# Attention scores of a hybrid streaming encoder: from two 64-row products per head to one 128-row product with both halves of the keys stacked

## The chip, the cores and the metric

The kernel runs on one core of one Trainium2 chip. The metric is the time of one execution on the device, in microseconds (us). The core has a matrix engine (PE, TensorE), whose weight loads the profile lists apart as PEld, a vector engine (DVE), a scalar engine (ACT), a slower general engine (POOL, GpSimd) and a queue that issues DMAs (SP). Each engine runs its own instructions in order and waits on semaphores for the others. On-chip working memory (SBUF) has 128 partitions; matrix products land in eight banks of PSUM.

## The reference

Two layers. In each, 1024 frames of a new stream (the prompt) and 32 frames of a running stream (the sample) are normalised, projected by one wide matrix and fed to three branches: A, a gated mixing inside chunks of 128; B, sliding-window attention with 8 query heads that share 2 key heads; C, chunk-band attention with 4 heads over the own chunk of 64 and 8 chunks before it. Gates multiply the branch outputs, and a second projection, a normalisation and a residual follow. Head width is 64. What the change touches is this (for the prompt):

```python
def block_attention(q, k, v, bias, valid, sinks):
    s = jnp.einsum('bnqhgd,bnlhd->bnhgql', q, k) * (HEAD_DIM ** -0.5) + bias
    if valid is not None:
        s = jnp.where(valid[None, :, None, None, None, :], s, NEG_INF)
    if sinks is None:
        p = jax.nn.softmax(s, axis=-1)
    else:
        m = jnp.maximum(jnp.max(s, axis=-1, keepdims=True), sink)
        e = jnp.exp(s - m)
        p = e / (jnp.sum(e, axis=-1, keepdims=True) + jnp.exp(sink - m))
    return jnp.einsum('bnhgql,bnlhd->bnqhgd', p, v)
```

## The kernel before

**Precision.** PE multiplies a rounded 32-bit format (float32r, printed fp32r) at full rate. To keep the accuracy of float32, an operand x is split into a high part (x rounded) and a low part (x minus the high part); `split` (line 420) does this with a copy on ACT or DVE and a subtraction on DVE or POOL. A product of two split operands is the sum of high by high, high by low and low by high: three matmuls.

**Stages.** A layer has two. In the first, 24 blocks of 128 projection columns (named `bq0`, `ck1`, `cz0` and so on; the order is written out in `ORDERS`, line 40) are computed for three token ranges of 384, 384 and 288 columns (`TOK`): 24 dense matmuls of 128 rows each, into one of three accumulator banks `d`, evacuated by `evac` (line 593). Queries are evacuated, scaled by 1/8, into the big tile `Y`, two heads of 64 on the 128 partitions. Keys are evacuated into a tile `v`, stored, and split (line 613) into `kt[:, 0]` (high) and `kt[:, 1]` (low), again two heads on the partitions. Gate blocks (`bz`, `cz`) are evacuated only when the attention of their pair is done. In the second stage the output projection runs over the three token ranges.

**Attention.** It is woven into the first stage. A `Unit` (line 650) is one pair of heads and a run of query blocks of 128: four blocks in branch B, two in C (`NQ`, line 53), so 8 units of B and 8 of C in a layer. Block q sees 1 or 2 key tiles of 128 in B and 1 to 5 in C. A unit has these steps:

- `Q(h)`: split of 256 query columns (two blocks) of both heads.
- `scores` (line 751): both heads j = 0, 1 from partitions 0 to 63 and 64 to 127, each into its own bank `S` (there are two), three matmuls of 64 rows each, alternating between the heads (`mm_s`, `both`). In B one call does two blocks, in C one; with five key tiles a call `tails` does the second half of the keys. Then DVE adds the bias and takes the minimum of the negated score (the op shows as CUSTOM_DVE_ANT_0), and `softmax` does the exponential on ACT, the sum with the sink in B, a reciprocal and a scaling.
- `T(g)`: transposes of the probabilities by PE into a bank `pt`, split into `ph` and `pl`. The last one of a head releases its score tiles `s`.
- `PV(g)`: products with the values into `pv`; at the end one half is copied to a tile `ot` by ACT and added to the other by DVE into `Y`.

Score tiles `s` come from a ring of 6 (`BUFS`, line 63); B takes 2 for two blocks, C 2 for a block.

**Order.** The whole program is written out by a planner when it is built: `Clock` (line 87) keeps an assumed time for each engine and buffer, steps wait in lanes (`LANES`, line 69), and `pump` (line 1118) takes a step when its assumed time has come, and otherwise lets the next dense matmul go. Nothing is reordered at run time. All engine instructions pass through one helper, so nearly every row of the profile has its line, L282, and is told apart by its tiles: `S<-kk,qh` is a score product with the high part of the queries, `d<-hh,whi` a dense one.

Of the kernel before, what the change touches and what calls it, by code (L numbers as in the profile page):

```python
# [40 lines left out]
    "bk bv bq0 cv0 bq1 ck1 bq2 bq3 av1 bz2 ck0 av0 cq0 cv1 cq1 az0 au0 bz0 bz1 bz3 az1 au1 cz1 cz0".split(),  # L41
    "bk bv bq0 bq2 bq1 ck1 bq3 cv0 av0 bz2 ck0 av1 cq0 cv1 au0 bz1 cq1 az0 bz0 cz0 bz3 az1 au1 cz1".split(),
# [21 lines left out]
    tmp=3, v=5, r=3, wraw=3, whi=3, wlo=3, kk=2, vv=2, ks=3, vs=3, s=6, qh=2, ql=2, ph=2, pl=2,  # L64
    nm=3, sm=3, sx=2, rd=3, ot=1, bias=3, t5=1, d=3, S=2, pt=2, pv=1,
# [4 lines left out]
    "wload store evac ysplit wsplit x h0 sq0 h1 sq1 h2 sq2 bnd0 bnd1 bnd2 xl lc t5 bias p t sb a vt sc q s"  # L70
# [227 lines left out]
def encoder(  # L298
# [158 lines left out]
    sk4 = cp.tile([128, 4, 2, 2], F32, name="sk4")  # L457
# [135 lines left out]
    def evac(l, n, t, d):  # L593
# [8 lines left out]
        elif ty == "k" or (ty == "v" and br != "a"):  # L602
# [47 lines left out]
    class Unit:  # L650


        def __init__(self, l, br, pair, qp):
# [23 lines left out]
            self.qh, self.ql, self.s, self.pt = {}, {}, {}, {}  # L677
# [3 lines left out]
        def steps(self):  # L681
            l, u = self.l, self
            halves = self.nq // 2
            for h in range(halves):
                end = self.c0 + 256 * h + 255
                tok = end // 384
                q = f"{l}.{self.br}q{self.pair}.{tok}"
                src = Y[:, self.blk, end - 255 : end + 1]
                lane("q").put(lambda h=h: self.Q(h), lambda q=q: q in done and free("qh") and free("ql"),
                              lambda src=src: max(after("act", [src]), slot("qh", "act")), f"{self.id}.Q{h}")  # L690
                need = marks(f"{self.id}.Q{h}", *(f"{l}.{self.k}.{t}" for t in range(tok + 1)), f"{l}.{self.br}{self.pair}.bias")
                parts = self.parts(h)
                for i, (p, fresh) in enumerate(parts):
                    done_h = i == len(parts) - 1

                    def part(p=p, h=h, done_h=done_h):
                        p()
                        if done_h:
                            let_go(u.qh[h], u.ql[h])
                            if u.end and h == halves - 1:  # L700
# [724 lines left out]
```

## Time and profile before

| | |
|---|---|
| time, median of 3 runs | 1029.36 us (1028.28 to 1031.23) |
| time of the profiled execution | 1028.7 us |
| its span, first to last instruction | 1027.0 us |
| mean granted clock of PE, share of full speed | 0.995 |
| busy: PE, DVE, ACT, POOL | 98%, 70%, 50%, 6% of the span |
| chain of work that ended last, by engine | PE 72%, DVE 13%, ACT 8%, issue 4%, DMA 2% |

How to read what follows. In a timeline a row has the start in us, a duration in us, engine, line, operation, the tiles as out<-in, the part of the array used and the shape of the moving operand, and a count of merged instructions. Matmuls are pipelined: their durations overlap, and what one costs is the distance from its start to the next start. A row of windows has the stretch in us, its length, then for PE, PEld, DVE, ACT and POOL the busy time and in brackets the number of instructions, then the granted clock of PE as a share of 2.4 GHz, the busy share of the DMA engines, and GB/s. A row of one tile has the count, durations in ns as min/median/max, first and last start in us, and the shapes. A row of groups has the count, then total busy us and mean ns of one, then the idle time before and who ended it.

### The profile page before, as it was taken

The page shows a single profiled execution, that of the slowest core. Times are in us where ns is not written, and L with a number is a line of the kernel's source. Part 1 is how long each engine was busy: PE and PEld are TensorE (multiplying, and loading weights), DVE is VectorE, ACT ScalarE, POOL GpSimd, SP SyncE. Part 2 cuts the span into 40 slices and gives each one's busy share as a digit, 9 for nine tenths or more (in the row PEclk, how much of TensorE's full clock was granted, in tenths as well). Part 3 has the DMA queues.
Part 4 walks back from the last instruction along what each step waited for, and adds up shares of the span by engine and source line. Part 5 has one row for each costly group of instructions (what it writes and reads, how often), then busy time and mean ns, then how long its engine had stood idle before and what let it go on. Part 6 is the DMA issues. An engine that isn't in the chain of part 4 may idle for free.

```text
span 1027.0 us, 18406 instructions
## 1 busy us (share of the span) xinstructions
PE 1003.7 (98%) x6842; PEld 951.4 (93%) x6842; DVE 715.6 (70%) x1849; ACT 509.5 (50%) x1300; POOL 66.6 (6%) x146
## 2 busy tenths in 40 slices
PE   8999999999999999999999999999999999999995
PEld 7899999988999999999988989899889899999995
DVE  8676777757677745857977687776676776566655
ACT  7465556435555512645744555653564454246331
POOL 0200100110000000000010010001100000000000
PEclk9999999999999999999999999999999999999998
DMA  8211111101100311435542110201011003126633
GB/s 279 44 55 43 43 42 47 53 21 39 63 21 22 114 42 63 157 119 183 161 125 67 32 56 29 68 22 61 25 32 57 32 21 94 41 83 196 190 101 120
DMA packets 52634, 78.63 MB, mean 77 GB/s; under 512 B 7104, under 2 KB 28992, under 8 KB 52544
## 3 DMA queue, kind: packets, MB, share of 16 engines
q1 hardware_dynamic: 52544, 77.45, 24.3%
q8 instruction: 54, 0.88, 0.4%
q14 instruction: 36, 0.29, 0.1%
HBM read 66.11 MB, written 11.31 MB: 75 GB/s over the span
## 4 chain that ended last, share of the span: by engine, by line
PE 72%; DVE 13%; ACT 8%; issue 4%; DMA 2%; POOL 0%; SPq 0%; POOLq 0%; ACTq 0%; DVEq 0%
PE d L282 47%; PE S L282 12%; PE pt L282 7%; PE pv L282 5%; ACT s L282 4%; DVE Y L282 3%; DVE pl L282 2%; DVE v L282 1%; DVE s L282 1%; DVE kk L282 1%; DVE wlo L282 1%; ACT ph L282 1%; DVE hl L282 1%; DMA wraw<-in_wo_dram 1%; ACT ot L282 1%
## 5 line engine op out<-in xcount | busy, mean ns | idle before, releaser
L282 PE MATMUL d<-hh,whi 128*128 128x384 f32 (+1 forms) x1132 | 382.4, 338 | 0.1
L282 PE MATMUL d<-hh,wlo 128*128 128x384 f32 (+1 forms) x1132 | 365.9, 323 | 0.8 <-DVE wlo L282 0.7
L282 PE MATMUL d<-hl,whi 128*128 128x384 f32 (+1 forms) x1132 | 364.9, 322 | 0.0
L282 PEld LDWEIGHTS d<-hh,whi 128*128 128x128 f32 x1132 | 213.0, 188 | 13.9 <-issue 8.4
L282 PEld LDWEIGHTS d<-hh,wlo 128*128 128x128 f32 x1132 | 212.7, 188 | 1.9 <-DVE wlo L282 1.9
L282 PEld LDWEIGHTS d<-hl,whi 128*128 128x128 f32 x1132 | 213.6, 189 | 0.0
L282 ACT ACTIVATE s<-s,nm 128x256 f32<-128x256 f32 (+5 forms) x196 | 107.8, 551 | 107.1 <-DVE nm L282 107.0
L282 DVE TENSOR_TENSOR pl<-pt,ph 128x512 fp32r<-128x512 f32 (+2 forms) x136 | 80.7, 623 | 18.0 <-ACT ph L282 17.6
L282 DVE TENSOR_TENSOR wlo<-wraw,whi 128x512 fp32r<-128x512 f32 x108 | 76.9, 714 | 6.5 <-ACT whi L282 5.0
L282 ACT ACTIVATE ph<-pt 128x512 fp32r<-128x512 f32 (+2 forms) x136 | 68.4, 541 | 23.3 <-PE pt L282 22.4
L282 ACT ACTIVATE whi<-wraw 128x512 fp32r<-128x512 f32 x105 | 65.2, 626 | 20.7 <-PE d L282 13.0
L282 PE MATMUL pv<-pl,vv 128*128 128x256 f32 (+1 forms) x288 | 70.2, 284 | 2.0 <-DVE pl L282 2.0
L282 ACT ACTIVATE ot<-pv 64x256 f32<-64x256 f32 x96 | 36.3, 378 | 71.1 <-PE pv L282 37.7
L282 PE MATMUL pv<-ph,vv 128*128 128x256 f32 (+1 forms) x288 | 70.2, 272 | 1.3 <-ACT ph L282 1.1
L282 ACT ACTIVATE tmp<-tmp 128x384 f32<-128x384 f32 (+1 forms) x48 | 23.9, 498 | 88.5 <-DVE tmp L282 85.0
L282 PE MATMUL pt<-ident,s 128*128 128x128 f32 x488 | 67.6, 274 | 0.0
L282 DVE TENSOR_TENSOR Y<-pv,ot 64x256 f32<-64x256 f32 x96 | 40.4, 421 | 36.2 <-ACT ot L282 35.2
L282 DVE CUSTOM_DVE_ANT_0 s<-S,bias,nsink 128x256 f32<-128x256 f32 (+1 forms) x128 | 52.1, 464 | 9.5 <-PE S L282 6.7
L282 DVE TENSOR_TENSOR v<-v,tmp 128x384 f32<-128x384 f32 (+1 forms) x80 | 41.7, 522 | 24.4 <-ACT tmp L282 23.3
L282 PEld LDWEIGHTS pv<-pl,vv 128*128 128x128 f32 x288 | 54.4, 189 | 3.9 <-DVE pl L282 3.6
L282 PEld LDWEIGHTS pt<-ident,s 128*128 128x128 f32 x488 | 56.0, 140 | 1.4 <-DVE s L282 0.2
L282 PEld LDWEIGHTS pv<-ph,vv 128*128 128x128 f32 x288 | 54.4, 189 | 2.7 <-ACT ph L282 1.8
(169 smaller groups left out, 1677.8 us busy)
## 6 DMA issues: line engine op xcount, KB each, us to landing
wraw<-in_w_dram SPq DMA_DIRECT2D x96, 256.0 KB, 2.7
wraw<-in_wo_dram SPq DMA_DIRECT2D x72, 256.0 KB, 3.0
x_d<-Y SPq DMA_DIRECT2D x16, 192.0 KB, 3.2
out_y_dram<-Y SPq DMA_DIRECT2D x16, 192.0 KB, 3.8
Y<-in_xT_dram SPq DMA_DIRECT2D x5, 576.0 KB, 6.1
bias<-fc_d SPq DMA_DIRECT2D x8, 320.0 KB, 4.3
s<-in_xT_dram SPq DMA_DIRECT2D x12, 192.0 KB, 3.2
s<-x_d SPq DMA_DIRECT2D x12, 192.0 KB, 3.9
```

Source lines behind the costliest of these rows:

```text
L282: return f(*args, **kw)
```

## The change

Scores use the full height of the array. For each head j the key tile holds the high part on one half of the partitions and the low part on the other: `kt[own, j]` and `kt[other, j]`. The queries of a head are put on both halves by four DMAs (`D`, in a new lane `qd`), from `Y` into the first 256 columns of the score tile that the block will use anyway, and split there. One matmul with the queries' high part then gives high by high plus high by low, and a second with the low part adds low by high and low by low: two matmuls of 128 rows instead of three of 64. All steps are per block of 128 queries: the split, the scores (in B both heads in one bank, in C one head at a time, with one or two banks) and the softmax. `softmax`, `tails` and `both` go into `scores`. A block takes its score tiles (one in B, two in C) when its query DMAs are issued. Besides, the copy before the last addition of `PV` goes to the shared ring `tmp` instead of `ot`, `qh` and `ql` have 3 buffers instead of 2, `v` 4 instead of 5, the expanded sink tile `sk4` is gone, and `ORDERS` is another.

```diff
@@ ORDERS @@
-    "bk bv bq0 cv0 bq1 ck1 bq2 bq3 av1 bz2 ck0 av0 cq0 cv1 cq1 az0 au0 bz0 bz1 bz3 az1 au1 cz1 cz0".split(),
-    "bk bv bq0 bq2 bq1 ck1 bq3 cv0 av0 bz2 ck0 av1 cq0 cv1 au0 bz1 cq1 az0 bz0 cz0 bz3 az1 au1 cz1".split(),
+    "bk bv bq0 bq1 cv0 ck1 bq2 cq0 av1 bq3 bz2 av0 cq1 ck0 bz3 az0 bz0 cv1 au1 au0 az1 bz1 cz0 cz1".split(),
+    "bk bv bq0 bq1 bq2 cv0 ck1 av0 bq3 av1 bz2 ck0 cq0 cq1 bz0 au1 cv1 bz1 au0 az1 az0 bz3 cz1 cz0".split(),
@@ BUFS @@
-    tmp=3, v=5, ... qh=2, ql=2, ... ot=1, ...
+    tmp=3, v=4, ... qh=3, ql=3, ...
@@ evac, keys @@
-                split(kt[:, 0, a : a + P], kt[:, 1, a : a + P], x[:, :P])
+                for j in (0, 1):
+                    own, other = slice(64 * j, 64 * j + 64), slice(64 - 64 * j, 128 - 64 * j)
+                    split(kt[own, j, a : a + P], kt[other, j, a : a + P], x[own, :P])
@@ Unit @@
+        def D(self, q):
+            c = self.c0 + 128 * q
+            self.t[q] = [tl([128, 640], "s") for _ in range(1 if self.br == "b" else 2)]
+            self.qr[q] = self.t[q][0][:, 0:256].rearrange("p (j c) -> p j c", j=2)
+            src = Y[:, self.blk, c : c + 128]
+            for j in (0, 1):
+                for i in (0, 1):
+                    dma.dma_start(self.qr[q][64 * i : 64 * i + 64, j, :], src[64 * j : 64 * j + 64, :])
+
-        def Q(self, h):
-            c = self.c0 + 256 * h
-            self.qh[h] = tl([128, 256], "qh", F32R)
-            self.ql[h] = tl([128, 256], "ql", F32R)
-            split(self.qh[h], self.ql[h], Y[:, self.blk, c : c + 256])
+        def Q(self, q):
+            self.qh[q] = tl([128, 2, 128], "qh", F32R)
+            self.ql[q] = tl([128, 2, 128], "ql", F32R)
+            split(self.qh[q], self.ql[q], self.qr[q])
         def mm_s(self, dst, j, q, c0, c1):
...
-            yield lambda: pe.matmul(dst, qh[sl, qs], kt[sl, 0, lo + c0 : lo + c1], start=True, stop=False)
-            yield lambda: pe.matmul(dst, qh[sl, qs], kt[sl, 1, lo + c0 : lo + c1], start=False, stop=False)
-            yield lambda: pe.matmul(dst, ql[sl, qs], kt[sl, 0, lo + c0 : lo + c1], start=False, stop=True)
+            k = st[self.l, self.k][:, j, 128 * self.lo[q] + c0 : 128 * self.lo[q] + c1]
+            pe.matmul(dst, self.qh[q][:, j, :], k, start=True, stop=False)
+            pe.matmul(dst, self.ql[q][:, j, :], k, start=False, stop=True)
+        def parts(self, q):
             if self.br == "b":
-                return [(lambda: self.scores((2 * h, 2 * h + 1)), True)]
...
+                return [(lambda: self.scores(q, (0, 1)), 1)]
+            return [(lambda j=j: self.scores(q, (j,)), 1 if self.n[q] <= 4 else 2) for j in (0, 1)]
+        def scores(self, q, js):
+            s = self.t[q][js[0]]
...
+            for c in range(0, n, m):
+                bank = ps("S")
+                for i, j in enumerate(js):
+                    dst = bank[:, 256 * i : 256 * i + m]
+                    self.mm_s(dst, j, q, c, c + m)
...
             if self.br == "b":
-                dve.tensor_tensor(sx, nm, sk4[:, self.pair, :, :].rearrange("p j q -> p (j q)"), ALU.add)
-                act.activation(sx, sx, AF.Exp)
-                dve.tensor_tensor(sm, sm, sx, ALU.add)
+                dve.tensor_tensor(sx[:, :2], nm[:, :2], sinkb[:, self.pair : self.pair + 5 : 4], ALU.add)
+                act.activation(sx[:, :2], sx[:, :2], AF.Exp)
+                dve.tensor_tensor(sm[:, :2], sm[:, :2], sx[:, :2], ALU.add)
             rd = tl([128, 4], "rd")
-            dve.reciprocal(rd[:, :nb], sm[:, :nb])
-            for b, k in enumerate(blocks):
-                scale(self.s[k], rd[:, b : b + 1])
+            dve.reciprocal(rd[:, :2], sm[:, :2])
+            for j in (0, 1):
+                scale(self.s[j, q], rd[:, j : j + 1])
@@ PV @@
-                    ot = tl([128, 256], "ot")
+                    ot = tmp()[:, :256]
```

## Rows read from the trace of the kernel before

**Rows 1.** The page, busy time, share of the span and instructions of each engine.

```profile
PE 1003.7 (98%) x6842; PEld 951.4 (93%) x6842; DVE 715.6 (70%) x1849; ACT 509.5 (50%) x1300; POOL 66.6 (6%) x146
```

**Rows 2.** Windows: attention of layer 0, dense rest, attention of layer 1, dense rest.

```profile
45.60:362.60 317.00, 314.13 (x2249) 291.31 (x2249) 226.18 (x669) 169.53 (x465) 23.05 (x57) 1.00 0.16 48
365.30:414.50 49.20, 49.20 (x312) 49.20 (x312) 27.26 (x52) 12.00 (x26) 0.20 (x1) 1.00 0.17 54
532.10:874.60 342.50, 339.31 (x2414) 316.11 (x2414) 244.45 (x705) 176.34 (x480) 23.05 (x43) 1.00 0.15 46
874.60:916.70 42.10, 42.10 (x269) 41.61 (x268) 23.61 (x46) 11.49 (x25) 2.59 (x2) 1.00 0.15 51
```

**Rows 3.** One tile, the queries' high part, whole span.

```profile
L282 PE MATMUL S<-kk,qh x448: 270/307/502, 45.6 to 854.9; 64*128 64x256 f32 x81, 64*128 64x320 f32 x44, 64*128 64x128 f32 x15, 64*128 64x384 f32 x6
L282 ACT ACTIVATE qh<-Y x42: 399/404/420, 29.3 to 806.5; 128x256 fp32r<-128x256 f32 x42
L282 DVE TENSOR_TENSOR ql<-Y,qh x40: 410/423/456, 30.9 to 816.2; 128x256 fp32r<-128x256 f32 x40
```

**Rows 4.** Timeline of PE, a call of B's scores between dense matmuls.

```profile
130.02 0.34 PE L282 MATMUL d<-hh,wlo 128*128 128x384 f32 x1
130.29 0.50 PE L282 MATMUL S<-kk,qh 64*128 64x256 f32 x4
...
131.19 0.44 PE L282 MATMUL d<-hh,whi 128*128 128x384 f32 x1
131.47 0.34 PE L282 MATMUL d<-hl,whi 128*128 128x384 f32 x1
131.64 0.34 PE L282 MATMUL d<-hh,wlo 128*128 128x384 f32 x1
```

**Rows 5.** Timeline of PE, a call of C's scores on 320 keys.

```profile
749.83 0.29 PE L282 MATMUL d<-hh,wlo 128*128 128x288 f32 x1
750.05 0.56 PE L282 MATMUL S<-kk,qh 64*128 64x320 f32 x4
750.45 0.31 PE L282 MATMUL S<-kk,ql 64*128 64x320 f32 x2
750.69 0.40 PE L282 MATMUL d<-hh,whi 128*128 128x288 f32 x1
750.92 0.29 PE L282 MATMUL d<-hl,whi 128*128 128x288 f32 x1
751.06 0.30 PE L282 MATMUL d<-hh,wlo 128*128 128x288 f32 x1
```

**Rows 6.** Timeline of PE, four products with the values between dense matmuls.

```profile
336.86 0.34 PE L282 MATMUL d<-hh,wlo 128*128 128x384 f32 x1
337.03 0.28 PE L282 MATMUL pv<-ph,vv 128*128 128x256 f32 x1
...
337.50 0.34 PE L282 MATMUL d<-hh,whi 128*128 128x384 f32 x1
337.68 0.34 PE L282 MATMUL d<-hl,whi 128*128 128x384 f32 x1
```

**Rows 7.** One tile, the keys: the low part, whole span.

```profile
L282 DVE TENSOR_TENSOR kk<-v,kk x18: 425/559/1524, 27.0 to 701.1; 128x384 fp32r<-128x384 f32 x12, 128x256 fp32r<-128x256 f32 x6
```

**Rows 8.** Groups by line, the softmax's reciprocal.

```profile
L282 DVE RECIPROCAL rd<-sm 128x4 f32<-128x4 f32 (+2 forms) x70 | 12.0, 171 | 37.9 <-ACT s L282 34.8 <-ACT vv L282 1.8
```

**Rows 9.** Timeline of the SP queue, eight small DMAs one after another.

```profile
25.16 3.68 SPq L282 DMA_DIRECT2D ssk<-in_sinks_dram  x8
```

**Rows 10.** DMA issues: count, KB each, median us from issue to landing.

```profile
bias<-fb_d SPq DMA_DIRECT2D x16, 20.0 KB, 2.6
ssk<-in_sinks_dram SPq DMA_DIRECT2D x16, 0.1 KB, 1.7
```

**Rows 11.** Timeline of PE, transposes that free four score tiles, then scores.

```profile
105.12 0.95 PE L282 MATMUL pt<-ident,s 128*128 128x128 f32 x7
106.00 0.50 PE L282 MATMUL S<-kk,qh 64*128 64x256 f32 x4
```

More of the change, by code (lines that the diff above doesn't have):

```diff
@@ L682, in steps, with part @@
             l, u = self.l, self
-            halves = self.nq // 2
-            for h in range(halves):
-                end = self.c0 + 256 * h + 255
+            for q in range(self.nq):
+                end = self.c0 + 128 * q + 127
                 tok = end // 384
[L687 to L696, printed above, removed]
-                        p()
-                        if done_h:
-                            let_go(u.qh[h], u.ql[h])
-                            if u.end and h == halves - 1:
+                there = f"{l}.{self.br}q{self.pair}.{tok}"
+                src = Y[:, self.blk, end - 127 : end + 1]
+                tiles = 1 if self.br == "b" else 2
+                lane("qd").put(lambda q=q: self.D(q), lambda there=there, tiles=tiles: there in done and free("s", tiles),
+                               lambda src=src, tiles=tiles: max(after("dma", [src]), slot("s", "dma", tiles)), f"{self.id}.D{q}")
+                lane("q").put(lambda q=q: self.Q(q), lambda d=f"{self.id}.D{q}": d in done and free("qh") and free("ql"),
+                              lambda q=q: max(after("act", [self.qr[q]]), slot("qh", "act")), f"{self.id}.Q{q}")
+                need = marks(f"{self.id}.Q{q}", *(f"{l}.{self.k}.{t}" for t in range(tok + 1)), f"{l}.{self.br}{self.pair}.bias")
+                parts = self.parts(q)
+                for i, (p, banks) in enumerate(parts):
+                    done_q = i == len(parts) - 1
+                    def part(p=p, q=q, done_q=done_q):
+                        p()
+                        if done_q:
+                            let_go(u.qh[q], u.ql[q])
+                            if u.end and q == u.nq - 1:
                                 let_go(*st[l, u.br, u.pair, "bias"])
@@ L703, in part @@
                                     let_go(st[l, u.k])
-                    lane("s").put(part, lambda fresh=fresh, need=need: need() and free("S", 2) and (not fresh or free("s", 2)),
-                                  lambda h=h: max(after("pe", [u.qh[h], u.ql[h]]), slot("S", "pe", 2)),
-                                  f"{self.id}.S{h}" if done_h else None, True)
+                    lane("s").put(part, lambda banks=banks, need=need: need() and free("S", banks),
+                                  lambda q=q, banks=banks: max(after("pe", [u.qh[q], u.ql[q]]), slot("S", "pe", banks)),
+                                  f"{self.id}.S{q}" if done_q else None, True)
             for i, g in enumerate(self.groups):
                 qs = {q for _, q0, n in g[1] for q in range(q0, q0 + n)}
-                vneed = marks(*(f"{self.id}.S{q // 2}" for q in qs))
+                vneed = marks(*(f"{self.id}.S{q}" for q in qs))
                 lane("t").put(lambda g=g: self.T(g), lambda vneed=vneed: vneed() and free("ph") and free("pl"),
```

90 lines of the change are left out of this document (27 added, 63 removed).

## The prediction

> **What bounds the kernel now.** I read the page's busy line first. The matrix engine (PE) is busy 98% of the span, the vector engine (DVE) 70%, the scalar engine (ACT) 50% [rows 1]. A busy PE need not be a PE that lacks time, so the second view is the windows. I cut each layer where its attention ends: from the first to the last attention matmul of layer 0 and of layer 1, and behind each the stretch of projection blocks that is left over before the output projection starts. In the attention stretches PE idles 317.00 - 314.13 = 2.9 us and 342.50 - 339.31 = 3.2 us, together 6.1 us, at a granted clock of 1.00 (the upper level, 2.4 GHz); DVE is busy 226.18 of 317.00 and 244.45 of 342.50 us, 71% in both [rows 2]. So PE's instruction stream sets the time: dense projection matmuls fill every hole that attention leaves, and a microsecond taken out of PE's stream is a microsecond off the end, as long as nothing else gets late. The other two windows are the cover for lateness: attention is finished 49.2 us before the dense blocks run out in layer 0, and 42.1 us in layer 1 [rows 2].
>
> The third view is the timeline of PE alone, because durations of matmuls overlap and only the distance from start to start is what one of them costs. There the scores show a price that no duration shows, at their two borders with the dense work; the next part takes it apart.
>
> **Score matmuls: removed and added.** The trace has 448 products with the high part of the queries [rows 3], and two of these go with one of the low part [rows 5], so 672 in all. By the code they come as 32 calls of branch B (12 each: two query blocks, two heads, three products) and 48 calls of branch C (6 each).
>
> A B call: the last dense start before it comes 0.27 us ahead of the first score where two dense neighbours of that size stand 0.17 apart, so 0.10 goes on the way in. From the first score to the next dense start it takes 131.19 - 130.29 = 0.90. The first dense step afterwards is 0.28 instead of 0.17, 0.11 on the way out [rows 4]. Sum 1.11 us. A C call on 320 keys: 0.22 against 0.14 on the way in, 750.69 - 750.05 = 0.64 inside, 0.23 against 0.14 on the way out [rows 5]. Sum 0.08 + 0.64 + 0.09 = 0.81 us.
>
> The new scores contract over all 128 rows, in the form that the probability-times-value products have now: 128 rows, rounded f32, two products in a row into the same bank. Four of these on 256 columns between dense neighbours take 337.50 - 337.03 = 0.47, that is 0.1175 each, and the dense steps on both sides stay at 0.17 and 0.18 [rows 6]: no price at the borders. A B call becomes 8 such products (two blocks, two heads, two products): 8 x 0.1175 = 0.94. Saved 1.11 - 0.94 = 0.17 a call, 32 x 0.17 = 5.4 us. A C call of 6 on 320 columns becomes 4. At 320 columns the step lies halfway between 0.1175 for 256 [rows 6] and 0.17 for 384 [rows 4], 0.147 by the slope: 4 x 0.147 = 0.59. Saved 0.81 - 0.59 = 0.22, 48 x 0.22 = 10.6 us; the 16 C calls of other widths are taken at the same saving, since the borders make it up. Together 16.0 us. All of it is border: inside, 0.94 replaces 0.90 and 0.59 replaces 0.64.
>
> Here a rule of the Trainium skill stands against the change. "TensorEngine Tiling (Array Packing)", section Overview, gives products with at most 64 rows up to twice the throughput, since two sit side by side in the array; going to 128 rows gives that up. By it alone the 12 old products would be six slots of 0.1175, 0.71 us, and the change would cost 8 slots, 0.94: +0.23 x 32 for B and, in the same way, +0.15 x 48 for C, 14.6 us slower. The trace does not bear that out at the level of a call: 0.90 plus borders, not 0.71. The same page, section Key Properties, says that a change of tiling mode drains the engine, and the 0.10 and 0.11 at the borders agree. The sum goes by the rows.
>
> **Query splits.** Before, 48 splits of 256 columns, one for two blocks; after, 96 of 256 columns, since each block now stands on both halves. 48 more high parts at 0.404 us, mostly on ACT, and 48 more low parts at 0.423 us, mostly on DVE [rows 3]: 19.4 us on ACT, 20.3 on DVE.
>
> **Key splits.** Each of 18 becomes two, of half the partitions and the same columns. A row of DVE costs 0.56 [rows 7]; taking high and low part alike, 18 x 2 x 0.56 = 20 us more. If fewer partitions were quicker it would be zero; no row shows that, so I keep 20.
>
> **Softmax per block.** Exponentials and bias additions keep count and width. For B the sink's two small additions and the reciprocal come 64 times instead of 32: 32 x 3 x 0.171 [rows 8] = 16 us on DVE, plus 32 small exponentials on ACT.
>
> DVE gets 20 + 20 + 16 = 57 us, 28 in each attention stretch, which is itself 8 us shorter: (226 + 28) / 309 = 82% and (244 + 28) / 334 = 82%, from 71%. ACT goes from 170 to about 183 of 309. Neither passes PE; the cover is PE's dense work. But the handover waits behind the 6.1 us of PE idle grow when the queues are fuller. If they go as busy over idle share, 0.71/0.29 = 2.4 becomes 0.82/0.18 = 4.6, and 6.1 becomes 11.5: plus 5 us. Bounds: nothing, or three times that (15).
>
> **The query DMAs.** 96 blocks x 4 = 384 new DMAs on the SP queue, behind which weight loads wait. Eight small ones took 3.68 us there, 0.46 each [rows 9], so four take 1.8; small ones land 1.7 to 2.6 us after issue [rows 10]. With the split, 0.4 + 0.4, a block's queries are ready 4.3 to 5.2 us after its tile comes free; I take 4.8. SP's queue grows by 177 us; in its own list of waits it mostly waits for a free weight buffer, so this is hidden, and weight loads, of which three are buffered, stand behind a query DMA that waits for its tile or for the evacuated queries. On ACT the query split now waits for the landing, and behind it stand exponentials and weight splits, for which PE waits in turn; the planner places it by an assumed landing time. If that time is kept, the chain alone matters: the score tile (6 of them) is now taken before the DMA. Today the score follows the last transposes that free its tile at once (transposes from 105.12, score at 106.00) [rows 11]; in the timeline the same happens once per pair of heads in B and once per unit in C, 4 + 8 = 12 times a layer. The 4.8 us come in there: 12 x 4.8 = 58 us of lateness a layer, less what the finer blocks give back. The cover is 49.2 + 8 = 57 and 42.1 + 8 = 50. I price it at nothing in the sum, with little to spare.
>
> The reordered blocks, the copy through the shared temporary instead of its own tile, and one buffer less for evacuated rows change no instruction's cost; each lies under dense work and gets zero, with an unknown of a few us either way that is inside the bounds above.
>
> **Sum.** The profiled execution took 1028.7 us (span 1027.0, the rest around it), 0.7 below the median of 1029.36. 1028.7 - 16.0 + 5 = 1017.7; beside the median 1018.4. I say 1018.
>
> **Rivals.** (a) *Vector work eats the gain.* PE's idle grows by 15 instead of 5: 1028.7 - 16 + 15 = 1028. For it: DVE is already the releaser of handovers, and 82% is an average over busier stretches. Against: only 6.1 us idle at 71%. Chance 0.17, of which 0.08 still faster, 0.07 same, 0.02 slower.
> (b) *The borders stay.* If the 0.2 us per call comes with any change to another operand pattern and not with the 64-row form, the change does not do what it says: 16.0 falls to 48 x 0.05 - 32 x 0.04 = 1, and about 1028 without any growth of waits, 1033 with it. Against: [rows 6] has none. Chance 0.06, mostly same.
> (c) *Attention comes too late; slower.* Place: the last heads of branch C, whose gate blocks end each layer and hold the accumulator banks until attention is there. Price: 4.8 us per exposed refill. It decides from 12 refills in layer 0 (57 us) and 10 in layer 1 (50 us) on; beyond, PE idles one for one. With 14 refills a layer, 67 us: 10 + 17 = 27 us lost, 1018 + 27 = 1045; 16 in each would lose 20 + 27. For it: [rows 11], and the cover matches the need so nearly. Against: two tiles of six are free for the next unit's first blocks; one block's softmax is a shorter chain than two's. Chance 0.17: 0.15 slower, 0.01 same, 0.01 faster. "DMA: Bandwidth & Descriptors", Rules for kernel authors, in the Trainium skill advises against two transfers to disjoint halves of the partitions, since they share the same engines and serialize; no run before shows such a pair. By it the four transfers of a block would land one behind another, which only lengthens the wait that (c) needs.
>
> **How the numbers follow.** A measurement of this kernel tells about 0.3%, 3 us, from no change. Forecast 0.60, all faster, its own range 1009 (no growth of waits, somewhat fewer than today) to 1025; (a) 0.17, (b) 0.06, (c) 0.17. Faster 0.60 + 0.08 + 0.01 + 0.01 = 0.70; same 0.07 + 0.05 + 0.01 = 0.13; slower 0.02 + 0.15 = 0.17. The range reaches up through (a) and (b) and the mild part of (c): 1009 to 1036.
>
> **What would show it.** In the changed profile, dense steps beside a score should be 0.17 and 0.14 with nothing added, and four 320-column products should take 0.59. PE idle inside attention should be 6 to 15 us, DVE near 82% there. The dense-only stretches behind attention should shrink but remain; if they are gone and PE waits before the output projection, (c) holds. Key splits much below 0.56 would make DVE's load too high here. The forecast fails if PE idle takes over 16 us more than today, wherever it stands.

## The result, and the profile after

The changed kernel takes 1081.14 us (1079.40 to 1081.39, 4 runs) against 1029.19 us (1028.28 to 1031.23, 4 runs) before: a ratio of 1.0494, 95% interval 1.0481 to 1.0506. It is 5% slower; forecast were 1018 us and a range of 1009 to 1036. The page's busy line of the changed kernel, beside [rows 1]:

```profile
PE 1025.0 (95%) x6618; PEld 981.1 (91%) x6618; DVE 763.9 (71%) x2038; ACT 522.7 (48%) x1363; POOL 66.7 (6%) x152
```

and its chain of work that ended last, by engine:

```profile
PE 47%; DVE 22%; ACT 9%; issue 8%; DMA 6%; SPq 5%; POOL 1%; DVEq 0%; ACTq 0%; POOLq 0%
```

DVE's busy share looks unchanged, but PE's part of the chain fell from 72% to 47%: the end is no longer set by PE's stream alone. The windows that answer to [rows 2] (attention, dense rest, attention, dense rest):

```profile
54.00:430.00 376.00, 356.55 (x2331) 338.86 (x2331) 263.50 (x782) 180.90 (x506) 26.09 (x62) 0.97 0.21 61
432.50:446.00 13.50, 13.50 (x88) 13.50 (x88) 10.53 (x21) 6.22 (x15) 0.00 (x0) 1.00 0.22 79
571.00:942.00 371.00, 356.18 (x2358) 336.41 (x2357) 269.82 (x803) 182.73 (x510) 23.13 (x47) 0.99 0.21 59
947.80:969.80 22.00, 22.00 (x139) 22.00 (x139) 13.36 (x26) 7.85 (x18) 0.00 (x0) 1.00 0.20 60
```

PE idles 376.00 - 356.55 = 19.5 and 371.00 - 356.18 = 14.8 us inside attention, 34.3 where it was 6.1; the prediction named 16 us more as its sign of failing. The covers behind attention shrank to 13.5 and 22.0 us, but they are still there.

The borders did go. A C call on 320 keys between dense matmuls, in PE's timeline (for [rows 5]):

```profile
332.91 0.34 PE L282 MATMUL d<-hh,wlo 128*128 128x384 f32 x1
333.08 0.31 PE L282 MATMUL S<-kk,qh 128*128 128x320 f32 x1
333.23 0.31 PE L282 MATMUL S<-kk,ql 128*128 128x320 f32 x1
333.37 0.31 PE L282 MATMUL S<-kk,qh 128*128 128x320 f32 x1
333.52 0.31 PE L282 MATMUL S<-kk,ql 128*128 128x320 f32 x1
333.67 0.34 PE L282 MATMUL d<-hh,whi 128*128 128x384 f32 x1
333.85 0.34 PE L282 MATMUL d<-hl,whi 128*128 128x384 f32 x1
```

From start to start: 0.17 in, four products in 333.67 - 333.08 = 0.59, then 0.18, as forecast. Over all calls of this trace the median step is 0.174 behind a dense matmul into a score and 0.175 behind the first dense start after it, so the borders are gone and the loss lies elsewhere.

Three views say where. First, the windows again, each attention stretch cut where the scores of branch C begin; the kernel before:

```profile
45.60:222.60 177.00, 174.13 (x1259) 163.25 (x1258) 127.25 (x395) 94.43 (x290) 16.38 (x35) 1.00 0.17 48
222.60:362.60 140.00, 140.00 (x991) 128.06 (x991) 98.92 (x276) 75.09 (x175) 6.67 (x22) 1.00 0.15 48
532.10:724.10 192.00, 189.01 (x1363) 178.38 (x1362) 141.49 (x425) 99.28 (x302) 16.45 (x28) 1.00 0.16 47
724.10:874.60 150.50, 150.30 (x1054) 137.73 (x1054) 102.96 (x281) 77.05 (x178) 6.60 (x15) 1.00 0.14 44
```

and the changed one:

```profile
54.20:249.80 195.60, 181.99 (x1182) 172.22 (x1181) 139.50 (x463) 95.02 (x305) 15.90 (x38) 0.97 0.24 65
249.80:430.00 180.20, 174.35 (x1150) 166.62 (x1151) 124.00 (x320) 85.88 (x201) 10.19 (x24) 0.97 0.19 56
571.10:781.40 210.30, 196.62 (x1286) 183.22 (x1284) 156.73 (x503) 102.38 (x325) 15.31 (x31) 0.98 0.22 62
781.40:942.00 160.60, 159.46 (x1071) 153.08 (x1072) 112.99 (x300) 80.25 (x186) 7.83 (x16) 1.00 0.20 56
```

Before, nearly all of PE's idle time in attention stood in B (2.9 and 3.0 us; C had 0.0 and 0.2). After, the B windows have 13.6 and 13.7, of which 2.7 is the wait of C's first score in layer 0 for its split keys; C has 5.9 and 1.1. Second, the SP queue at the start of the run, where 12 query DMAs stand ahead of the first layer's constants and 12 more ahead of the last of these; in the kernel before the transfers to `tmp`, to `fb_d` and the first ones to `bias` were issued at 34.98, 44.10 and 46.03 us:

```profile
28.51 7.55 SPq L282 DMA_DIRECT2D s<-Y  x12
...
45.47 0.32 SPq L282 DMA_DIRECT2D tmp<-in_crel_dram  x1
...
49.43 7.53 SPq L282 DMA_DIRECT2D s<-Y  x12
...
59.04 0.30 SPq L282 DMA_DIRECT2D fb_d<-tmp  x1
...
62.68 1.74 SPq L282 DMA_DIRECT2D bias<-fb_d  x4
```

Third, the granted clock. Its mean fell from 0.995 to 0.978, and windows on the stretches in which it fell show 0.50 (1.2 GHz), 37.4 us together; before there is none between 10.4 us and the end phase.

```profile
48.30:58.50 10.20, 9.42 (x36) 7.79 (x37) 2.13 (x6) 1.30 (x3) 0.73 (x1) 0.50 0.21 48
72.20:75.60 3.40, 3.40 (x16) 3.40 (x16) 2.58 (x11) 1.49 (x6) 0.00 (x0) 0.50 0.02 5
...
584.20:594.40 10.20, 8.83 (x37) 8.57 (x38) 5.40 (x17) 2.65 (x9) 1.12 (x1) 0.50 0.36 94
```

From 72.2 to 75.1 us a dense step on 288 columns takes 0.24, where it takes 0.13 at full clock (444.87 to 445.00). So these stretches hold up to 37.4 / 2 = 19 us of the loss, an estimate, as the second half of a price whose first half is a wait of PE: each of the six stands behind one.

### The profile page after: what moved, and what is told of

Its sections match the earlier page's. It is cut to its first block, busy times and chain, and to the rows that moved or that the text cites. A ratio compares the mean times of both kernels' runs of the same rounds, so it can differ in the third digit from the quotient of the medians.

```text
span 1079.6 us, 19235 instructions
## 1 busy us (share of the span) xinstructions
PE 1025.0 (95%) x6618; PEld 981.1 (91%) x6618; DVE 763.9 (71%) x2038; ACT 522.7 (48%) x1363; POOL 66.7 (6%) x152
## 4 chain that ended last, share of the span: by engine, by line
PE 47%; DVE 22%; ACT 9%; issue 8%; DMA 6%; SPq 5%; POOL 1%; DVEq 0%; ACTq 0%; POOLq 0%
PE d L282 29%; PE S L282 9%; SPq L282 5%; DVE s L282 5%; ACT s L282 5%; PE pt L282 5%; PE pv L282 4%; DVE Y L282 4%; DMA s<-Y 3%; DVE pl L282 3%; DVE wlo L282 2%; DVE v L282 2%; ACT tmp L282 1%; DMA wraw<-in_wo_dram 1%; DVE kk L282 1%
## 5 line engine op out<-in xcount | busy, mean ns | idle before, releaser
L282 PE MATMUL d<-hh,wlo 128*128 128x384 f32 (+1 forms) x1144 | 372.0, 325 | 1.2 <-DVE wlo L282 0.7
L282 PE MATMUL d<-hl,whi 128*128 128x384 f32 (+1 forms) x1144 | 370.3, 324 | 1.2 <-DVE hl L282 1.2
L282 PEld LDWEIGHTS d<-hh,whi 128*128 128x128 f32 x1144 | 217.4, 190 | 8.5 <-DVE whi L282 2.9
L282 PEld LDWEIGHTS d<-hh,wlo 128*128 128x128 f32 x1144 | 217.2, 190 | 3.3 <-DVE wlo L282 3.3
L282 PEld LDWEIGHTS d<-hl,whi 128*128 128x128 f32 x1144 | 218.4, 191 | 1.8 <-DVE hl L282 1.7
L282 PE MATMUL pv<-pl,vv 128*128 128x256 f32 (+1 forms) x288 | 74.3, 298 | 4.8 <-DVE pl L282 4.4
L282 PE MATMUL S<-kk,qh 128*128 128x256 f32 (+3 forms) x224 | 69.0, 320 | 9.5 <-DVE nm L282 3.5
L282 ACT ACTIVATE ph<-pt 128x512 fp32r<-128x512 f32 (+2 forms) x136 | 67.7, 539 | 11.9 <-PE pt L282 10.7
L282 PE MATMUL S<-kk,ql 128*128 128x256 f32 (+3 forms) x224 | 65.5, 308 | 2.9 <-DVE ql L282 2.1
L282 ACT ACTIVATE tmp<-pv 64x256 f32<-64x256 f32 x96 | 36.4, 380 | 59.8 <-PE pv L282 29.9
L282 PEld LDWEIGHTS pv<-pl,vv 128*128 128x128 f32 x288 | 55.9, 194 | 10.4 <-DVE pl L282 9.6
L282 DVE TENSOR_TENSOR Y<-pv,tmp 64x256 f32<-64x256 f32 x96 | 40.3, 420 | 30.5 <-ACT tmp L282 29.6
```

The costliest lines, as they stand in the source:

```text
L282: return f(*args, **kw)
```

## The experiments

Theories: **(V)** the added vector work (key splits, query splits, small sink operations) delays handovers in B; **(Q)** the query DMAs make what stands behind them on SP late; **(O)** the new order of blocks and the finer steps leave PE without work. In nearly all runs "order kept" means that the planner's clock is still told of the old operations, so that each remaining instruction keeps its place in the program. Then the n-th PE instruction is the same in two traces, and subtracting their starts shows where a difference arises. The kernel before ran beside each: 1029.1 to 1030.1 us.

**1. Full-height scores alone, in the kernel before** (the planner's bookkeeping is left out of this cut).

```diff
-  pe.matmul(dst, qh[sl, qs], kt[sl, 0, ...]); pe.matmul(dst, qh[sl, qs], kt[sl, 1, ...]); pe.matmul(dst, ql[sl, qs], kt[sl, 0, ...])
+  nc.tensor.matmul(dst, qh[:, qs], kt[:, j, ...]); nc.tensor.matmul(dst, ql[:, qs], kt[:, j, ...])
```

> The kernel before, with nothing changed but the score products: two over all 128 rows for each head instead of three over 64, in the order that the planner wrote for the old ones. The queries are not put on both halves and the keys not stacked, so the scores mix two heads and the output is not the reference's. If the borders with the dense work were the price of the 64-row form, as the sum of the prediction has it, 16 us come off: about 1013 us. If the border price comes with any change of operands, the time stays within 3 us of 1029.

Measured 1020.98 us, ratio 0.9918 (0.9899 to 0.9937): 8.4 us faster where the prediction has 16.0, between the two bands expected. Windows of the two attention stretches, up to where each one's products with the values end:

```profile
45.50:361.10 315.60, 311.67 (x2156) 299.70 (x2155) 227.97 (x672) 169.92 (x466) 22.83 (x58) 1.00 0.16 48
528.40:870.40 342.00, 337.44 (x2320) 326.55 (x2320) 243.33 (x705) 176.29 (x480) 22.91 (x43) 1.00 0.15 46
```

Idle 3.9 + 4.6 = 8.5 us (6.1 before). PE's instructions other than the scores are the same in both traces, in the same order, so the starts can be subtracted call by call. From the start of the instruction before a call to the second start behind it, the 80 calls lose 14.8 us in all: 9.5 on the way in, 8.3 on the way out, and 3.0 more than before inside. The way in got shorter behind transposes too: 43 calls stand behind dense matmuls (the median step falls from 0.268 to 0.173, 3.9 us in all), 31 behind work into the bank `pt` (5.1 us), 6 behind products with the values (0.6). So nearly the whole 16.0 was there at the calls. Outside of them the stream of this execution gets 7.5 us longer again: 4.0 of that between products with the values, whose operands DVE and ACT split, 2.5 at transposes and on the way into these products, 1.5 in one stretch at half clock. Half of what was taken out of PE's stream arrived at the end (7.3 us in this execution, 8.4 by the medians).

**2. The parts taken out of the changed kernel**, one by one and together, order kept.

```diff
 (no query DMAs: the split reads Y itself)
-  dma.dma_start(self.qr[q][...], src[...])   # x4
-  split(self.qh[q], self.ql[q], self.qr[q])
+  split(self.qh[q], self.ql[q], Y[:, self.blk, c : c + 128].unsqueeze(1).to_broadcast([128, 2, 128]))
 (key splits whole)
-  for j in (0, 1): split(kt[own, j, ...], kt[other, j, ...], x[own, :P])
+  split(kt[:, 0, ...], kt[:, 1, ...], x[:, :P])
 (no sinks in B)
-  dve.tensor_tensor(sx[:, :2], nm[:, :2], sinkb[...], ALU.add)
-  act.activation(sx[:, :2], sx[:, :2], AF.Exp)
-  dve.tensor_tensor(sm[:, :2], sm[:, :2], sx[:, :2], ALU.add)
```

No query DMAs:


> The changed kernel in its own order, instruction for instruction, without the 384 query DMAs: the split reads the queries of both heads straight from the big tile, so the scores mix two heads. Queue theory (query DMAs hold up the SP queue and with it weights, bias tables and queries): most of the 52 us come back, 1045 us or less. Vector theory (more work on the vector engine, which hands over late): at most 10 us come back, 1071 or more. Plan theory (the new written order itself makes PE wait, whatever the single costs are): less than 10 as well.

Keys whole and no sinks:


> The changed kernel in its own order with its DMAs, without the added vector work on keys and sinks: the keys are split as before, 18 pairs over all partitions instead of 36 over half of them, and the sink's part of the sums in branch B is left out (its two additions on the vector engine and its exponential on the scalar engine, 64 times). Scores mix two heads and the sums lack the sink. Vector theory: 20 us or more come back, 1061 or less. Queue theory: less than 10, above 1071. Plan theory: less than 10.

All three:


> The two removals before this together: no query DMAs, keys split as before, no sink in branch B; order as in the changed kernel. If queue and vector work together are the cause, this runs at about the time that the cheaper score products promise, 1010 to 1025 us. If the order is the cause, it stays above 1050.

Keys whole alone:


> After, with its instruction order kept, but each key piece is split once, whole (18 pairs of 128 rows), instead of twice on 64 rows; the sinks and the query DMAs stay. Left out: the low parts stand where the plain kernel had them, so the scores mix the two heads. Together with the sinks' additions this was worth 24.6 us (1081.1 to 1056.5). Theory that the key splits carry it, since they are long (0.51 us), come in a burst after each key block and PE was seen to wait 3.0 us behind one of them: 1081 - 16 = 1065 (1062 to 1069). Theory that the sinks' small additions carry it, since they lie in the chain from score to softmax and were the largest new wait of the vector engine: 1081 - 7 = 1074 or more.

All three, and the query split on 128 columns:


> The kernel without query DMAs, without doubled key splits and without the sinks (1036.8 us), with its order kept, where the queries are now also split on 128 columns per block instead of 256: the vector and scalar engine split as many columns as before the change, in twice as many instructions. Left out besides: both heads' products use the same query tile half. Theory that vector work sets what is left of the loss (16 us over the kernel before with full rows, 1020.8): 96 x about 0.15 us less on each of the two engines, 8 to 12 us back, 1025 to 1029. Theory that the rest is the order and the finer steps: 1033 to 1037.

| left out of the changed kernel | us | ratio to before (95%) | back |
|---|---|---|---|
| query DMAs | 1061.49 | 1.0309 (1.0286 to 1.0332) | 19.7 |
| doubled key splits, sinks | 1056.52 | 1.0257 (1.0226 to 1.0288) | 24.6 |
| all three | 1036.77 | 1.0074 (1.0053 to 1.0095) | 44.4 |
| doubled key splits | 1073.05 | 1.0420 (1.0399 to 1.0440) | 8.1 |
| all three, doubled query splits | 1028.71 | 0.9986 (0.9977 to 0.9995) | 52.4 |

The effects add up (19.7 + 24.6 = 44.3). Without the query DMAs the time stands between the bands of the theories, and so does it without all three: no theory holds alone. For the key splits both theories missed: 8.1, not 16, so the sinks hold 24.6 - 8.1 = 16.5, by subtraction; no run left out the sinks alone. Doubled query splits: 1036.8 - 1028.7 = 8.1, as theory V expected. Starts of the same matmuls, changed kernel against the one without doubled key splits and sinks: 1.6 us apart at 109 us, 12.2 at 254, 11.3 at 437, 13.4 at 557, 25.3 at 796, 25.2 at the end. Nothing is lost in C or in the dense rests: 22 of the 25 us arise in the B windows, 2.1 between the layers. Against the kernel without query DMAs: 11.5 apart already at 88 us, 11.9 at 229, 14.9 at 463, 18.5 at 841.

**3. What the sinks cost before, and another way to add them.** The kernel of experiment 1 without its 32 sets of sink operations; and the kernel before with the sink as one more column behind each head's scores, so that the exponential's own sum takes it in.

```diff
-  dve.tensor_tensor(sx, nm, sk4[...], ALU.add); act.activation(sx, sx, AF.Exp); dve.tensor_tensor(sm, sm, sx, ALU.add)
+  nc.gpsimd.tensor_copy(ts_[j][:, at + n : at + n + 1], nsink[...])   # second kernel only, ahead of the exponential
```

> Before, order kept, with scores as two products of 128 rows (1021.0 us), and without the sinks' additions and exponential in branch B, which here are one set for two blocks (32) instead of one for each (64). Left out: the sinks, and the scores mix two heads. It does the same vector work as the kernel after change that lost query DMAs, doubled key splits, sinks and doubled query splits (1028.7). Theory that the sinks cost 17 us in the changed kernel because there are twice as many: here half of that, 1021 - 8 = 1013 (1011 to 1015), and 16 us are left for order, finer steps and buffers. Theory that the sinks cost only where the queues are already late: 1019 to 1021, and 8 us are left.

> Before, order and scores kept, nothing left out: the sink is written by POOL as one more column behind each head's scores, ahead of the exponential, so that the exponential's own sum takes it in; the two additions and the small exponential fall away. Theory that the chain from score to softmax is where vector work costs: 4 to 8 us faster, 1021 to 1025. Theory that it costs only where the queues are late: 1027 to 1030.

The first: 1014.18 us, ratio 0.9851 (0.9837 to 0.9866), 6.8 us below experiment 1 and inside the band of the theory that the price goes with the number. A set costs 6.8 / 32 = 0.21 us there and 16.5 / 64 = 0.26 in the changed kernel, so it does so roughly; 16.5 - 6.8 = 9.7 is what doubling added. The second: 1031.12, ratio 1.0010 (0.9995 to 1.0025), no gain. The groups of the second kernel, of the first and of the kernel before show first where DVE waits (after the last bar the idle time of DVE ahead of the instruction and who ended it; L799 is B's exponential in the second kernel):

```profile
L282 DVE RECIPROCAL rd<-sm 128x4 f32<-128x4 f32 (+2 forms) x70 | 12.0, 171 | 74.6 <-ACT s L799 37.8 <-ACT s L282 34.8 <-ACT vv L282 1.8
```

```profile
L282 DVE RECIPROCAL rd<-sm 128x4 f32<-128x4 f32 (+2 forms) x70 | 12.0, 172 | 66.1 <-ACT s L282 64.2 <-ACT vv L282 1.8
```

```profile
L282 DVE TENSOR_TENSOR sm<-sm,sx 128x4 f32<-128x4 f32 (+1 forms) x36 | 5.8, 162 | 29.2 <-ACT sx L282 29.2
```

DVE has to wait for ACT at the end of each softmax. Take away the addition at which it waited (29.2 us), and it waits at the reciprocal instead: 34.8 us there before, 64.2 in the first kernel, 37.8 + 34.8 in the second. But the first kernel gained 6.8 us in spite of this, so the move of the wait is not why the second did not. What only the second has is POOL's 128 copies, for which B's exponential waits. Starts of the same matmuls, second kernel against before, show two places at which it loses 3.5 and 4.5 us; everywhere else it gains, about 5 us in all. The second place, ACT and then PE:

```profile
173.94 0.51 ACT L799 ACTIVATE s<-s,nm 128x257 f32<-128x257 f32 x1 [4.88 <-POOL s L767]
```

```profile
176.76 1.35 PE L282 MATMUL pt<-ident,s 128*128 128x128 f32 x5 [2.82 <-ACT s L282]
```

At the first, ACT waits 7.25 us for POOL up to 52.42, and PE 2.46 up to 57.01; behind both waits of PE stand 3.4 us at half clock. So the sinks' operations cost this kernel too, and this way of adding them pays it back through POOL; a way without POOL in the chain was not tried. In the changed kernel DVE's wait comes once for each block of B:

```profile
DVE sm L282 <- ACT sx L282: 46.9, 68, 1.0
```

68 times where it was 36 (64 and 32 of them are the sets of sinks).

**4. Where the query DMAs cost.** The kernel before with the 384 DMAs added, to memory that nobody reads; the changed kernel with all of them, and with the constants of layer 0, on POOL's queue.

```diff
+  nc.sync.dma_start(spare_q[n, 64 * i : 64 * i + 64, j, :], Y[64 * j : 64 * j + 64, self.blk, b : b + 128])   # added to before
-  dma.dma_start(self.qr[q][...], src[...])
+  dmb.dma_start(self.qr[q][...], src[...])        # all on POOL
-  dma.dma_start(fb_d, f[:8, :FB_W])
+  dmb.dma_start(fb_d, f[:8, :FB_W])               # constants on POOL (and the other tables)
```

> Before, order and all else kept, plus the four query DMAs of each block, issued on the same queue just ahead of the query split, to a scratch in memory that nobody reads. Nothing waits for their landing. Theory that the issue time on that queue is what costs (0.63 us each, 242 us in all, behind which weight loads and constants stand): slower by 8 to 20 us, 1037 to 1049. Theory that the queue has room and that only the wait for the landing, ahead of the split, costs: 1029 to 1032.

> After, order kept, with the query DMAs issued from the queue of the general engine (POOL), which is busy 6% of the span, instead of the queue that carries weights, constants and stores. Nothing is left out. Theory that the loss of 20 us from these DMAs is the queue behind them: most of it comes back, 1081 - 15 = 1066 (1062 to 1070). Theory that it is the wait of the split for the landing: 1079 to 1083, or slower, since additions and subtractions on POOL now stand behind a DMA that waits for its tile.

> After, order kept, nothing left out: the constants of layer 0 that stand behind the first query DMAs (the two relative-bias tables on their way through memory, the first bias tables) are issued from POOL's queue; the query DMAs stay where they are. Theory that the cost of the query DMAs is mostly that constants of the first layer come 10 us late: 1081 - 10 = 1071 (1069 to 1073). Theory that it is spread over the run, weight loads above all: 1078 to 1082.

Added to before: 1045.31, ratio 1.0151 (1.0131 to 1.0171), 15.6 us with nothing waiting for a landing. All on POOL: 1087.56, ratio 1.0555 (1.0530 to 1.0580). Its starts are 9.3 to 11.1 us ahead of the changed kernel's around 100 us, and it loses them again, because a quarter of the low parts of the queries is computed on POOL, and PE now waits for these (PE's waits; 0.5 us in the changed kernel):

```profile
PE S L282 <- POOL ql L282: 12.5, 5, 3.6
```

Constants on POOL: 1079.01, ratio 1.0480 (1.0462 to 1.0499), which decides nothing: POOL's own order made them wait for earlier constants that were still on SP, and the first table was issued at 47.60 us, later than the 45.47 of the changed kernel. So the first six blocks alone were moved, from the changed kernel to POOL's queue, and out of the kernel before with DMAs added:

```diff
-  dma.dma_start(self.qr[q][...], src[...])
+  (dmb if sent[0] <= 6 else dma).dma_start(self.qr[q][...], src[...])
```

> After, order kept, nothing left out: the query DMAs of the first six blocks only (24 of 384, ahead of the first layer's constants) are issued from POOL's queue, the other 360 from SP's as before. Theory that the queue costs only there, where nothing else keeps it waiting: 1081 - 9 = 1072 (1070 to 1074), more than half of what all 384 cost. Theory that it costs all through the run: 1079 to 1081.

> Before, order kept, with the unread query DMAs of the run that added all 384 (1045.3 us), but without those of the first six blocks: 360 of 384. Theory that the queue costs only at the start: 1045 - 8 = 1037 or less, the rest being one place at 295 us. Theory that it costs in proportion to the DMAs: 1044.

1071.45 us, ratio 1.0406 (1.0387 to 1.0426): these 24 of 384 DMAs carried 9.7 of the 19.7 us. And 1032.35, ratio 1.0035 (1.0022 to 1.0047): 13.0 of 15.6 us. (The traced execution with all DMAs added is the fastest of its four, 1042.0: there 8.3 of 13.1 us arise before 60 us, and 4.0 near 297 us, which the run without the first six blocks has too.) One place is six transposes of the normalisation factors `r`. PE's timeline in the kernel before, the changed one, the changed one with six blocks on POOL, and the kernel before with all DMAs; with those after the sixth block alone it is as in the kernel before (35.54, a wait of 0.33):

```profile
35.70 0.94 PE L282 MATMUL pt<-ident,r 128*128 128x128 f32 x6 [0.33 <-POOL r L282]
```

```profile
49.08 1.49 PE L282 MATMUL pt<-ident,r 128*128 128x128 f32 x6 [3.00 <-POOL r L282]
```

```profile
36.53 0.93 PE L282 MATMUL pt<-ident,r 128*128 128x128 f32 x6 [1.06 <-POOL r L282]
```

```profile
45.49 1.49 PE L282 MATMUL pt<-ident,r 128*128 128x128 f32 x6 [4.56 <-POOL r L282]
```

POOL computes `r` behind steps that wait for the constants, as its timeline in the changed kernel shows:

```profile
38.99 1.32 POOL L282 TENSOR_SCALAR_AFFINE_SELECT wt<-wt 128x128 f32<-128x128 f32 x4 [4.34 <-DMA wt<-in_aws_dram]
43.41 0.33 POOL L282 TENSOR_SCALAR nsink<-sinkb 128x8 f32<-128x8 f32 x1 [3.10 <-DMA sinkb<-in_sinks_dram]
47.29 0.23 POOL L282 TENSOR_SCALAR ssk<-ssk 128x2 f32<-128x2 f32 x1 [3.54 <-DMA tmp<-in_crel_dram]
...
48.16 0.86 POOL L282 TENSOR_TENSOR r<-r,mhalf 128x3 f32<-128x3 f32 x1
```

So the chain is: query DMAs on SP, constants behind them, POOL's steps behind the constants, `r` behind these, PE. In the kernel before with DMAs added this row and the 10.2 us at half clock behind it hold the whole 8.3. In the changed kernel they hold 7.4 of what the first six blocks cost up to 76 us (starts against the run with these on POOL), and 6.0 arise at a second place, with 3.4 us at half clock behind it: the bias tables, issued at 62.68, hold up DVE's first softmax of B and with it PE's next scores.

```profile
65.84 0.35 DVE L282 CUSTOM_DVE_ANT_0 s<-S,bias,nsink 128x128 f32<-128x128 f32 x1 [12.57 <-POOL bias L282]
```

```profile
66.68 0.39 PE L282 MATMUL S<-kk,qh 128*128 128x256 f32 x1 [0.90 <-DVE nm L282]
...
70.21 0.38 PE L282 MATMUL S<-kk,qh 128*128 128x256 f32 x1 [1.73 <-ACT qh L282]
```

**5. The new order alone**, in the kernel before; here the program is planned anew.

```diff
-  ORDERS = (order before)
+  ORDERS = (order after)
```

> Before with the changed kernel's order of projection blocks and nothing else; the rest of the program order follows from it. Theory that the new order costs what is left after the query DMAs and the vector work (8 to 16 us): 1037 to 1046. Theory that the finer steps cost it: 1027 to 1032.

Measured 1036.72 us, ratio 1.0079 (1.0058 to 1.0101): 7 us slower, just under the band that theory O gave. The changed kernel without its four added parts (1028.7) stands 14.5 us above the kernel before with full-height scores and no sinks (1014.2). The expectation ahead of experiment 3 took these two for equal in vector work. They are not: DVE is busy 722.6 us in the former and 702.9 in the latter, 19.7 more. The largest part is scaling of the probabilities, 32 of which the planner gave to DVE where ACT had them (24 left there, of 56); the latter's group, then the former's:

```profile
L282 DVE TENSOR_SCALAR s<-s,rd 128x256 f32<-128x256 f32 (+5 forms) x140 | 45.8, 371 | 2.4
```

```profile
L282 DVE TENSOR_SCALAR s<-s,rd 128x256 f32<-128x256 f32 (+5 forms) x172 | 57.6, 370 | 3.5
```

Another 4.9 us are the reciprocals, 102 instead of 70. Besides, the former has 13.6 us at half clock before the end phase and the latter none, up to 6.8 of the 14.5. One place can be named, the start of layer 1: PE's timeline of the former shows dense blocks waiting for the normalised input of the last token range,

```profile
548.36 0.40 PE L282 MATMUL d<-hh,whi 128*128 128x288 f32 x1 [0.89 <-ACT hh L282]
549.94 0.40 PE L282 MATMUL d<-hl,whi 128*128 128x288 f32 x1 [1.19 <-DVE hl L282]
...
551.87 0.61 PE L282 MATMUL d<-hh,whi 128*128 128x288 f32 x1 [1.40 <-DVE hh L282]
```

and DVE's timeline there has the softmax of B's first blocks between those normalisations, each with a wait for ACT:

```profile
545.53 0.17 DVE L282 RECIPROCAL rd<-sm 128x2 f32<-128x2 f32 x1 [0.76 <-ACT s L282]
...
547.91 0.17 DVE L282 RECIPROCAL rd<-sm 128x2 f32<-128x2 f32 x1 [0.75 <-ACT s L282]
...
549.11 0.78 DVE L282 SCALAR_TENSOR_TENSOR hl<-Y,g_sb,hh 128x288 fp32r<-128x288 f32 x1
```

These waits and the 6.8 us at half clock behind them (from 551.2 us on) come to 3.5 + 3.4, about 7 us, an estimate. The rest was not taken apart: neither the moved scalings nor the finer steps nor the buffers were tried by themselves. No kernel here that keeps all of the computation beats the kernel before.

## Why the prediction was wrong

| term | predicted | measured at the end | from |
|---|---|---|---|
| borders and scores | -16.0 | -8.4 (-14.8 at the calls) | experiment 1 |
| key splits | in the +5 | +8.1 | 2 |
| doubled sinks | in the +5 | +9.7 | 2 and 3 |
| doubled query splits | in the +5 | +8.1 | 2 |
| query DMAs | 0 | +19.7 | 2 and 4 |
| rest: order, finer steps, buffers, 19.7 us of DVE work | 0 | +14.5 | 2, 3 and 5 |
| sum | -11 | +51.7 | result: +51.9 |

That the sum closes is no proof of the terms: the last one is the distance that is left between two runs, so the column adds up as soon as the effects of experiment 2 do.

**The borders: the cost was right, the step to the end was not.** The calls and their borders lose 14.8 of the 16.0 us, more at the borders (17.8) than the samples gave, and 3.0 us dearer inside where the sum had 1.1 gained. What failed is "a microsecond taken out of PE's stream is a microsecond off the end": with vector work unchanged, half of it came back, most of that around the products with the values, whose operands come from DVE and ACT. (One slip of the sum: 0.147 for a 320-column product is 320/256 of 0.1175; halfway between 0.1175 and 0.17 is 0.144, which would have saved 0.6 us more over the 48 calls.) The rule of the Trainium skill that spoke against the change ("TensorEngine Tiling (Array Packing)", Overview, up to twice the throughput for products of at most 64 rows) did not decide: by the prediction's estimate from it full height would have cost 14.6 us, and experiment 1 gained 8.4.

**The vector work: mechanism right, size wrong, and the bounds too narrow (0 to 15 for 25.9 measured).** The low part of a key on 64 rows takes what one on 128 takes [rows 7], so half the rows save nothing:

```profile
L282 DVE TENSOR_TENSOR kk<-v,kk x36: 419/552/557, 26.3 to 771.4; 64x384 fp32r<-64x384 f32 x24, 64x256 fp32r<-64x256 f32 x12
```

The high parts were charged too much: a median of 0.352 us on DVE, not 0.56, and the added 18 run on ACT. All in all DVE's busy time grew by 763.9 - 715.6 = 48.3 us, not 57, and this holds 11.7 us of scalings that the forecast does not have. The three terms hold about 32 us of DVE time (9.4 by the run without doubled keys, half of 20.4 for the sinks, 12.4 for the query splits) and 22 of ACT's, and 25.9 arrived at the end.

What failed is the step "if they go as busy over idle share", with the share taken over the whole attention stretch. B and C are different stages, and nearly all of PE's idle time before stood in B. DVE is also kept from work by waiting for ACT in each softmax, which no busy share counts: in the B windows DVE's busy time and its 32 waits ahead of the sink's addition come to 127.3 + 141.5 + 26.1 = 295 of 369 us before, 80%, not 71%. That this wait is what made the term so large is argued, not shown; experiment 3 moves it without removing it. And the share did not rise to 82% afterwards, as a step of the forecast said it would: PE and DVE wait for each other, so the stretch grew with the work (in B 139.5 of 195.6 us, 71%, and 156.7 of 210.3, 75%).

**The query DMAs: the step that failed outright** is "SP's queue grows by 177 us; in its own list of waits it mostly waits for a free weight buffer, so this is hidden". That list is a sum over the run. At the start SP does not wait for buffers, it issues the first layer's constants, and half of the whole price arose there. In steady state the step was nearly right: the 360 later DMAs cost 3.3 us in the kernel before, most of it at one place (PE waits 0.72 and 0.92 us for a product with the values, up to 288.84, and 3.4 us at half clock follow). In the changed kernel they cost about 10; the 7 between are the landing and the order, which were not separated. The issue was also dearer than the 0.46 taken from the small ones: 7.55 / 12 = 0.63 us each, with 1.9 from issue to landing.

**Rival (c) named lateness, but the wrong place.** Attention did come later (covers 13.5 and 22.0 us instead of 49.2 and 42.1; the 42.1 count from 874.6, while the last product with the values ends at 877.3, so 39.4 compares with the others), yet PE never ran out of dense work behind it; it waited inside attention, on many handovers and not on 12 refills. **Rival (a)** had the right mechanism, with 15 us where 26 came from its terms. **Rival (b)** is out: the borders went. None of the cases held a loss of clock: 37.4 us at half rate belong to the measured terms of the table.

**What was not settled:** how the 14.5 us divide among order, finer steps, buffers and the work that the planner moved to DVE (the order alone gives 7 in the kernel before), and how much of each term is the wait itself and how much the slower clock behind it.

## What to carry to other kernels

When PE is 98% busy and its waits are small, a microsecond less for PE is not a microsecond off the end: half of 14.8 came through. Look for the stage in which the few waits stand, and cost added vector work there; here 26 us came through of about 32 on DVE. When a planner writes the program, compare afterwards what it gave to which engine. A DMA queue that is idle on average is not idle at the start: list what stands behind each new DMA in order, up to the engine that waits, and move just those (24 of 384 carried half the price). Before duplicating operands to make a matrix product denser, count the duplicate's splits and transfers: 8 us came off and 60 were paid.

## What the runs showed of the hardware

PE's granted clock fell to 0.50 behind waits that look harmless. In the changed kernel it fell in six places: at 48.3 us, in a wait of PE of 3.0 us that ends at 49.08, and at 584.2 us behind waits of 1.73, 1.19 and 1.40, for 10.2 us each; at 72.2 (behind 1.73 and 0.69), 116.6 (behind 2.19 and 0.34), 249.7 (in one of 2.66) and 277.0 (behind one of 2.62) for 3.4 or 6.8 us. With the unread DMAs added to the kernel before, which has no such stretch there, a wait of 4.56 us that ends at 45.49 went with 10.2 us at 0.50 from 44.8 us on; without the first six blocks' DMAs, waits of 0.72 and 0.92 us, up to 288.84, went with 3.4 us at 0.50 from 290.3 us on. Over most runs the mean clock rises as parts are taken out: 0.978 changed, 0.980 without doubled keys and sinks, 0.984 without DMAs too, 0.989 without doubled query splits, 0.994 in the kernel before with full-height scores and no sinks. It is not the same for all: without doubled keys alone it is 0.976, with the time 8.1 us shorter.

One more: inside a call, 64-row products of the two heads cost 0.90 / 12 = 0.075 us each on 256 columns [rows 4], where 128-row ones cost 0.1175 [rows 6]. They do run faster, 1.6 times; but there are 12 of them where 8 are needed at full height, 0.90 against 0.94 us, and the borders of 0.10 and 0.11 come on top.
